# Decoder trunk on one core: the ramp's loads on two queues with casts in tile order, the last columns' residual added in the bank, and the down projection's loads asked for in order of use

## The chip, the cores and the metric

The kernel runs on one core of a Trainium2 chip. The time is device microseconds of one execution, from the device's own clock; lower is better. The engines are TensorE (PE, matmuls into PSUM banks; PEld is its loading of weights), VectorE (DVE), ScalarE (ACT), GpSimd (POOL) and SyncE (SP). DMAs are issued by SP, ACT or POOL, each with a queue of its own.

## The reference

A hybrid decoder trunk of one layer: 256 tokens behind 16 meta tokens (T = 272), width 2048, all in float32. Cut to what matters:

```python
u = rmsnorm(h, norm_mix)
proj = u @ w_in                               # q, k, v, gates of two groups of heads
ret = head_norm(retention(...), ret_norm) * silu(g_r)
hm = head_norm(mlstm(...), mlstm_norm) * sigmoid(o_m)
h = h + concat([ret, hm]) @ w_out
u = rmsnorm(h, norm_ffn)
gate, val = split(causal_dwconv(u @ w_up, ffn_conv_w, ffn_conv_b))   # FFN_DIM = 5632
h = h + (silu(gate) * val) @ w_down
out = rmsnorm(h, norm_final)[meta tokens dropped]
```

## The kernel before

Every float32 operand of a product is split into two parts of a rounded format: `whi` is the weight cast by ACT (L121), `wlo` the rest, raw minus `whi`, by DVE (L123); likewise `xh` and `xl`, `mh` and `ml`. A product is three matmuls: high x high (L130), low x high (L131) and high x low (L133). Weights come from HBM into `wraw`, a pool of four slots that all stages share; a load waits for a slot until the cast and the subtraction of the slot's last user are done. `whi` and `wlo` have five slots each. PSUM gives four banks `mmps` and four banks `atps`. The order of the instructions on each engine is set by a scheduler of the language at build time, from its own estimate of durations, from dependences, and from orders that the code gives (`issue_after`, `high_priority`); at run time each engine and each queue goes through its list in that order and waits where a semaphore says so.

The stages are: a ramp that projects k, q and the gates of the first heads straight from the inputs; the rest of the input projection with the two groups of heads; the output projection; and then, in two halves of the hidden units, up projection, convolution and gate, and down projection.

The ramp: `WARM` matmuls of `ones` (L199) keep PE busy before the first data. Then for k = 0, 1, and pairs (2,3), (4,5), ... SP loads 128 rows of the transposed input (`hT`) and of the first weights (`w0`, into `wraw`; for k = 0 and 1 on ACT's queue), ACT scales and casts `xh` (L219) and casts the weights of the pair in one instruction (L224), DVE makes `xl` (L220), `wlo` (L226) and the last 64 columns of `whi` (L227); PE does eight matmuls for each k (L130 to L133, L235, L236). `par` holds the norm's gains, without which no `xh` can be made.

The down projection goes, in each half, over two blocks b = 0 and 2, of two column tiles of 512 (b and b+1) and two row tiles each, and in each block over 11 steps q of two hidden tiles. Four steps (q = 0, 4, 9, 10) are plain: their `wd` weights are loaded for each of the two column tiles (L118), cast and multiplied with all four row and column combinations in `atps` (L827 to L830). The other seven (q = 1, 2, 3, 5 to 8) form a 2 x 2 product from seven products (`seven`, L859 to L862): one part of the weights (`kept`, 256 KB, worked out earlier) and three from HBM (`wd7`, 768 KB) are loaded into one of two areas `left`, which lie in `hT`, in turn; DVE forms differences `ta` (L844) and `tb` (L845) in two `wraw` slots; `split` (L764 on ACT, L766 on DVE) casts four operands, two from `hT` and two from `wraw`. Behind a block its seven-product banks are combined (`share`: L884 to L895) and the `atps` banks copied (L951), and POOL adds both to `hn` by accumulating DMAs (`hn<-x`, L878). In the last block of the second half the steps come in another order, and the last four plain steps of the second column tile are kept back (`alone`), so that the row tiles end one after another.

The end: `add` (L900) adds a bank to the residual `hn`; `squares` (L694, ACT) sums the squares; `times_gain` (L698, POOL) multiplies by the last norm's gain; `gather` (L703, L704) and `finish` (L710 to L714) give the factor of the row, and `scale` (L721 with the gain, L723 without, L726 on ACT) and the DMAs `out` end the kernel. The last 512 columns of the second row tile are done as two halves of 256.

## Time and profile before

| | |
|---|---|
| median of 3 runs | 1207.33 us (1207.29 to 1207.91) |
| profiled execution | 1207.7 us, span 1205.9 us |
| PE, DVE, ACT, POOL busy | 1194.6, 971.5, 709.5, 162.8 us |
| mean DMA rate over the span | 218 GB/s |

The median and the profiled execution are different executions. The span runs from the first to the last event of the profile; 1.8 us of the profiled execution lie outside. A wait in the profile is a gap on one engine, put down to the semaphore that came last; a chain goes back from the last instruction to whatever released it.

### The profile page before, as it was taken

Reading aid. Unit: us, or ns where it says so; the run is one execution under the profiler, and the core shown is the slowest. Engines: PE = TensorE matmul, PEld = TensorE weight load, DVE = VectorE, ACT = ScalarE, POOL = GpSimd, SP = SyncE. Lnnn points to the kernel's source line nnn. Section 1 sums busy time; section 2 is a strip of 40 time slices with the busy share of each in tenths; the row PEclk is TensorE's granted clock in tenths of the full one; section 3 lists DMA queues with packets and bytes.
Section 4 is the critical chain, followed back from the end, with each engine's and each line's share of the span. In section 5 each row is a group of like instructions: output and inputs, shape, how many; then the busy total and the mean of one; then the engine's idle time right before and its main releaser. Section 6 shows DMA issues by size and latency. Waiting matters only on the chain.

```text
span 1205.9 us, 22794 instructions
## 1 busy us (share of the span) xinstructions
PE 1194.6 (99%) x8956; PEld 1151.2 (95%) x8956; DVE 971.5 (81%) x1444; ACT 709.5 (59%) x963; POOL 162.8 (14%) x223
## 2 busy tenths in 40 slices
PE   9999999999999999999999999999999999999997
PEld 9999999999999999999999998878999999998886
DVE  8968788766775966789889879897788778789897
ACT  8747656655656646555555557664555555556664
POOL 0100001111110311021122100202022112100232
PEclk9999999999999999999999999999999999999999
DMA  8765555666565965766766834959787777755956
GB/s 278 269 212 164 170 184 170 197 183 192 169 192 165 349 200 175 252 220 212 253 219 214 279 117 175 278 177 276 284 251 255 223 240 249 261 176 211 274 181 186
DMA packets 83004, 263.27 MB, mean 218 GB/s; under 512 B 14672, under 2 KB 18896, under 8 KB 82768
## 3 DMA queue, kind: packets, MB, share of 16 engines
q1 hardware_dynamic: 71952, 223.85, 57.0%
q0 software_dynamic: 10368, 37.11, 10.1%
q8 instruction: 70, 1.15, 0.4%
q10 hardware_dynamic: 576, 0.85, 0.2%
q14 instruction: 38, 0.31, 0.1%
HBM read 243.42 MB, written 11.27 MB: 211 GB/s over the span
## 4 chain that ended last, share of the span: by engine, by line
PE 96%; DMA 2%; DVE 1%; ACT 0%; issue 0%; SPq 0%; DVEq 0%; ACTq 0%
PE mmps L130 26%; PE mmps L131 25%; PE mmps L133 25%; PE atps L827 2%; PE atps L828 2%; PE atps L830 2%; PE mmps L860 2%; PE mmps L862 2%; PE mmps L859 2%; PE atps L862 1%; PE atps L860 1%; PE atps L859 1%; DMA hn<-x 1%; PE atps L379 1%; DMA hT<-in_wd 1%; PE atps L371 0%
## 5 line engine op out<-in xcount | busy, mean ns | idle before, releaser
L121 ACT CAST whi<-wraw 128x1024 fp32r<-128x1024 f32 x352 | 369.3, 1050 | 342.0 <-PE mmps L131 228.7
L123 DVE TENSOR_TENSOR wlo<-wraw,whi 128x1024 fp32r<-128x1024 f32 x352 | 432.3, 1230 | 72.5 <-ACT whi L121 70.0
L130 PE MATMUL mmps<-uh,whi 128*128 128x258 f32 x1408 | 346.1, 283 | 0.0
L131 PE MATMUL mmps<-ul,whi 128*128 128x258 f32 x1408 | 346.0, 283 | 0.0
L130 PEld LDWEIGHTS mmps<-uh,whi 128*128 128x128 f32 x1408 | 267.6, 190 | 0.1
L131 PEld LDWEIGHTS mmps<-ul,whi 128*128 128x128 f32 x1408 | 267.1, 190 | 0.1
L130 PE MATMUL mmps<-xh,whi 128*128 128x272 f32 (+2 forms) x864 | 219.8, 288 | 0.0
L131 PE MATMUL mmps<-xl,whi 128*128 128x272 f32 (+2 forms) x864 | 218.3, 286 | 0.0
L133 PE MATMUL mmps<-uh,wlo 128*128 128x258 f32 x1408 | 196.5, 282 | 0.0
L133 PEld LDWEIGHTS mmps<-uh,wlo 128*128 128x128 f32 x1408 | 179.9, 189 | 0.0
L131 PEld LDWEIGHTS mmps<-xl,whi 128*128 128x128 f32 x864 | 162.8, 188 | 0.0
L130 PEld LDWEIGHTS mmps<-xh,whi 128*128 128x128 f32 x864 | 162.5, 188 | 0.1
L133 PE MATMUL mmps<-xh,wlo 128*128 128x272 f32 (+2 forms) x864 | 126.7, 285 | 0.0
L133 PEld LDWEIGHTS mmps<-xh,wlo 128*128 128x128 f32 x864 | 114.2, 188 | 0.0
L680 DVE TENSOR_TENSOR cu<-mmps,rstd 128x258 f32<-128x258 f32 x88 | 37.4, 425 | 55.3 <-PE mmps L133 54.8
L764 ACT CAST whi<-hT 128x1024 fp32r<-128x1024 f32 x52 | 53.6, 1052 | 27.2 <-PE atps L828 7.3
L766 DVE TENSOR_TENSOR wlo<-hT,whi 128x1024 fp32r<-128x1024 f32 x52 | 62.1, 1220 | 4.9 <-ACT whi L764 3.7
L131 PE MATMUL mmps<-mixl,whi 128*128 128x258 f32 x256 | 63.0, 283 | 0.0
L130 PE MATMUL mmps<-mixh,whi 128*128 128x258 f32 x256 | 62.4, 282 | 0.0
L764 ACT CAST whi<-wraw 128x1024 fp32r<-128x1024 f32 (+1 forms) x52 | 43.0, 838 | 16.8 <-PE mmps L860 6.8
L766 DVE TENSOR_TENSOR wlo<-wraw,whi 128x1024 fp32r<-128x1024 f32 (+1 forms) x52 | 52.2, 1037 | 0.6 <-PE mmps L862 0.2
L827 PE MATMUL atps<-whi,mh 128*128 128x512 f32 (+1 forms) x132 | 50.9, 387 | 1.3 <-ACT whi L121 1.1
(280 smaller groups left out, 1700.1 us busy)
## 6 DMA issues: line engine op xcount, KB each, us to landing
wraw<-in_wu SPq DMA_DIRECT2D x176, 512.0 KB, 4.4
wraw<-in_wi SPq DMA_DIRECT2D x108, 512.0 KB, 4.1
hT<-in_wd SPq DMA_DIRECT2D x26, 768.0 KB, 4.7
wraw<-in_wd SPq DMA_DIRECT2D x36, 512.0 KB, 4.7
wraw<-in_wo SPq DMA_DIRECT2D x32, 512.0 KB, 4.2
x<-in_wd POOLq DMA_DIRECT2D x13, 768.0 KB, 7.0
hn<-x POOLq DMA_DIRECT2D x27, 256.0 KB, 7.9
hT<-kept SPq DMA_DIRECT2D x26, 256.0 KB, 2.9
```

What stands on the lines that cost most here:

```text
L121: nc.scalar.copy(hi, raw)
L123: nc.vector.tensor_tensor(out=lo, in0=raw, in1=hi.bitcast(F32), op=ALU.subtract)
L130: nc.tensor.matmul(ps, hi[:, k, :], xh(kk), start=kk == first, stop=False)
L131: nc.tensor.matmul(ps, hi[:, k, :], xl(kk), start=False, stop=False)
L133: nc.tensor.matmul(ps, lo[:, k, :], xh(kk), start=False, stop=kk == last)
L680: evacuated = nc.vector.tensor_tensor(out=u, in0=ps[:, :NQ], in1=rstd2, op=ALU.mult)
L764: copied = nc.scalar.copy(hi, x)
L766: return copied, nc.vector.tensor_tensor(out=lo, in0=x, in1=hi.bitcast(F32), op=ALU.subtract)
L827: nc.tensor.matmul(ps, ah[i], hi[:, i, cols], start=first and i == 0, stop=False)
L859: nc.tensor.matmul(o, sh[:, f, m, :], hi[:, i, :], start=begin, stop=False)
L860: nc.tensor.matmul(o, sl[:, f, m, :], hi[:, i, :], start=False, stop=False)
L862: nc.tensor.matmul(o, sh[:, f, m, :], lo[:, i, :], start=False, stop=end)
```

## The change

In the ramp, the loads of the first three groups (k = 0, 1 and the pair 2, 3) are asked for at the start: `hT` on SP, the weights and, behind the first, `par` on ACT's queue. The weights of k = 0 to 3 are cast tile by tile, each directly behind its `xh`; k = 0's cast is done by DVE. A one-column copy on ACT stands ahead of the first `xh`. `WARM` goes from 8 to 7, and the memset of `ones` is the first on DVE. In the down projection every load of a stage is asked for behind the one before it, in the order in which the steps use them (`asked`). At the end the bank `pa1` of the last 256 columns gets one matmul, then the residual by a DVE add (L994 in the new file), then the rest of its matmuls; ACT squares it where it stands and `finish` scales from it; the gain of the 256 columns ahead of it is applied in `scale`, not by POOL.

```diff
@@ -32,7 +32,7 @@
 W0 = GW + 2 * P
-WARM = 8
+WARM = 7
@@ -104,18 +104,17 @@
     inv_dm = consts.tile([P, P], F32, name="inv_dm")
-    nc.vector.memset(inv_dm, 1.0 / DM)
     epsc = consts.tile([P, 1], F32, name="epsc")
-    nc.vector.memset(epsc, EPS)
     rstd2 = consts.tile([P, NQ], F32, name="rstd2")
...
-    def load_w(src, shape, to=None):
+    def load_w(src, shape, to=None, after=None):
         nonlocal last_load
         raw = wpool.tile(shape, F32, name="wraw", bufs=4)
-        last_load = nc.sync.dma_start(raw, src)
+        with tc.issue_after(after.ins) if after else nullcontext():
+            last_load = nc.sync.dma_start(raw, src)
         to, n = (wpool, 5) if to in (None, wpool) else (to, None)
@@ -169,6 +168,8 @@
     nc.vector.memset(ones, 1.0)
+    nc.vector.memset(inv_dm, 1.0 / DM)
+    nc.vector.memset(epsc, EPS)
     inv_ret = pa.tile([P, P], F32R, name="inv_ret")
@@ -204,27 +205,41 @@
     with pool("sq", 1, side="right") as sqp:
-        for k0, k1 in [(0, 1), (1, 2)] + [(k, k + 2) for k in range(2, KT, 2)]:
+        chunks = [(0, 1), (1, 2)] + [(k, k + 2) for k in range(2, KT, 2)]
+
+        def ask(k0, k1):
+            nonlocal last_load
+            nc.sync.dma_start(hT[:, k0:k1, :], io["xT"][:, k0:k1, :])
+            raw = wpool.tile([P, 2, W0], F32, name="wraw", bufs=4)[:, : k1 - k0, :]
+            load = (nc.scalar if k0 < 4 else nc.sync).dma_start(raw, io["w0"][:, k0:k1, :])
+            if k0 == 0:
+                nc.scalar.dma_start(par[:, 0:KT], io["par"][:, 0:KT])
+            if k0 >= 4:
+                last_load = load
+            return raw, load
+
+        asked = {c: ask(*c) for c in chunks[:3]}
+        with tc.issue_after(asked[chunks[2]][1].ins):
+            copied = nc.scalar.copy(rstd1[:, 0:1], ones[:, 0:1])
+        for k0, k1 in chunks:
             n = k1 - k0
-            nc.sync.dma_start(hT[:, k0:k1, :], io["xT"][:, k0:k1, :])
-            if k0 == 0:
-                nc.sync.dma_start(par[:, 0:KT], io["par"][:, 0:KT])
...
-            for k in range(k0, k1):
-                nc.scalar.activation(xh[:, k, :], hT[:, k, :], AF.Copy, scale=pcol("gmix", k))
-                nc.vector.scalar_tensor_tensor(out=xl[:, k, :], in0=hT[:, k, :], scalar=pcol("gmix", k),
-                                               in1=xh[:, k, :].bitcast(F32), op0=ALU.mult, op1=ALU.subtract)
-
+            raw, _ = asked[k0, k1] if (k0, k1) in asked else ask(k0, k1)
             hi = wpool.tile([P, 2, W0 + GW], F32R, name="whi", bufs=5)[:, :n, :]
-            copied = nc.scalar.copy(hi[:, :, 0:W0], raw)
             lo = wpool.tile([P, 2, 2 * P], F32R, name="wlo", bufs=5)[:, :n, :]
-            nc.vector.tensor_tensor(out=lo, in0=raw[:, :, 0 : 2 * P], in1=hi[:, :, 0 : 2 * P].bitcast(F32), op=ALU.subtract)
-            parted = nc.vector.tensor_tensor(out=hi[:, :, W0:], in0=raw[:, :, 2 * P :], in1=hi[:, :, 2 * P : W0].bitcast(F32), op=ALU.subtract)
+            for c0, c1 in [(0, 1), (1, 2)][:n] if k0 < 4 else [(0, 2)]:
+                for k in range(k0 + c0, k0 + c1):
+                    with tc.issue_after(copied.ins) if k != 1 else nullcontext():
+                        nc.scalar.activation(xh[:, k, :], hT[:, k, :], AF.Copy, scale=pcol("gmix", k))
+                if k0 == 0:
+                    nc.vector.tensor_copy(hi[:, c0:c1, 0:W0], raw[:, c0:c1])
+                else:
+                    copied = nc.scalar.copy(hi[:, c0:c1, 0:W0], raw[:, c0:c1])
+                nc.vector.tensor_tensor(out=lo[:, c0:c1], in0=raw[:, c0:c1, 0 : 2 * P], in1=hi[:, c0:c1, 0 : 2 * P].bitcast(F32), op=ALU.subtract)
+                for k in range(k0 + c0, k0 + c1):
+                    with tc.issue_after(parted.ins) if k >= 2 else nullcontext():
+                        nc.vector.scalar_tensor_tensor(out=xl[:, k, :], in0=hT[:, k, :], scalar=pcol("gmix", k),
+                                                       in1=xh[:, k, :].bitcast(F32), op0=ALU.mult, op1=ALU.subtract)
+                parted = nc.vector.tensor_tensor(out=hi[:, c0:c1, W0:], in0=raw[:, c0:c1, 2 * P :], in1=hi[:, c0:c1, 2 * P : W0].bitcast(F32), op=ALU.subtract)
             for k in range(k0, k1):
@@ -703,7 +718,7 @@
-    def finish(tt, n):
+    def finish(tt, n, end=None):
@@ -713,12 +728,12 @@
         rows = slice(tt * P, (tt + 1) * P)
-        late = DM - 256 if n == 4 else DM - 512
+        late = DM - 512
...
             if c0 >= late:
-                nc.vector.scalar_tensor_tensor(out=h, in0=h, scalar=t, in1=gfin[:, c0:c1], op0=ALU.mult, op1=ALU.mult)
+                nc.vector.scalar_tensor_tensor(out=h, in0=h if end is None or c0 < DM - 256 else end, scalar=t, in1=gfin[:, c0:c1], op0=ALU.mult, op1=ALU.mult)
             else:
@@ -728,9 +743,8 @@
             nc.sync.dma_start(out[rows, c0:c1], hn[:, tt, c0:c1])
-        for c0, c1 in ((1536, late), (late, DM)):
-            if c0 < c1:
-                scale(c0, c1)
+        for c0, c1 in ((1536, DM),) if end is None else ((1536, 1792), (1792, DM)):
+            scale(c0, c1)
         nc.sync.dma_start(out[rows, 1536:], hn[:, tt, 1536:])
@@ -739,7 +753,7 @@
     left = hT.rearrange("p k t -> p (k t)")[:, 0:4096].rearrange("p (i a n) -> i p a n", i=2, a=4)
-    turn = 0
+    turn, asked = 0, None
@@ -811,7 +825,7 @@
-        def product(ps, tt, q, w, first=False, last=False, c0=0):
+        def product(ps, tt, q, w, first=False, last=False, c0=0, n0=0, n1=6, seed=False, seeded=False):
@@ -823,22 +837,21 @@
                           for m, a in zip((sh, sl), a21))
-            for i in range(2):
-                nc.tensor.matmul(ps, ah[i], hi[:, i, cols], start=first and i == 0, stop=False)
-                nc.tensor.matmul(ps, al[i], hi[:, i, cols], start=False, stop=False)
-            for i in range(2):
-                nc.tensor.matmul(ps, ah[i], lo[:, i, cols], start=False, stop=last and i == 1)
+            parts = [(a[i], hi, i) for i in range(2) for a in (ah, al)] + [(ah[i], lo, i) for i in range(2)]
+            for n, (a, m, i) in list(enumerate(parts))[n0:n1]:
+                nc.tensor.matmul(ps, a, m[:, i, cols], start=first and n == 0, stop=seed or last and n == 5, skip_group_check=seeded)
...
-            nonlocal turn
+            nonlocal turn, asked
             f = FAST.index(q)
...
-            nc.sync.dma_start(raw[:, 0, :], early[b, q])
-            nc.sync.dma_start(raw[:, 1:4, :], io["wd7"][b // 2, half * NQD + q][:, 1:4, :])
+            for to, src in ((raw[:, 0, :], early[b, q]), (raw[:, 1:4, :], io["wd7"][b // 2, half * NQD + q][:, 1:4, :])):
+                with tc.issue_after(asked.ins) if asked else nullcontext():
+                    asked = nc.sync.dma_start(to, src)
             ta, tb = (wpool.tile([P, 2, 512], F32, name="wraw", bufs=4) for _ in range(2))
@@ -909,8 +922,12 @@
         def load_step(b, q, to=wpool):
-            return load_w(io["wd"][b, half * NQD + q], [P, 2, 512], to)
-
+            nonlocal asked
+            w = load_w(io["wd"][b, half * NQD + q], [P, 2, 512], to, asked)
+            asked = last_load
+            return w
+
+        asked = None
         lag = 4
@@ -969,16 +986,21 @@
             add(cs[1, 1], 1, c)
-            for i in range(2):
-                p = at.tile([P, 512], F32, name="atps")[:, 0:256]
-                for q in sorted(ws):
-                    product(p, 1, q, ws[q], q == alone[0], q == alone[-1], c0=i * 256)
-                add(p, 1, c + i * 256)
-                squares(1, 3 + i, c + i * 256, c + (i + 1) * 256)
-                if i == 0:
-                    times_gain(1, c, c + 256)
-                    gather(1, 4)
-            finish(1, 4)
+            qs = sorted(ws)
+            pa0, pa1 = (at.tile([P, 512], F32, name="atps")[:, 0:256] for _ in range(2))
+            h = hn[:, 1, c + 256 : DM]
+
+            product(pa1, 1, qs[0], ws[qs[0]], True, c0=256, n1=1, seed=True)
+            nc.vector.tensor_tensor(out=pa1, in0=pa1, in1=h, op=ALU.add)
+            for q in qs:
+                product(pa0, 1, q, ws[q], q == qs[0], q == qs[-1])
+            add(pa0, 1, c)
+            squares(1, 3, c, c + 256)
+            gather(1, 4)
+            for q in qs:
+                product(pa1, 1, q, ws[q], False, q == qs[-1], c0=256, n0=1 if q == qs[0] else 0, seeded=True)
+            nc.scalar.activation(junk[:, 0:256], pa1, AF.Square, scale=DM ** -0.5, accum_out=ss4[:, 1, 4:5])
+            finish(1, 4, pa1)
```

What this does to the order of the instructions is shown at three places.

ACT at the start of the ramp, before (L215 loads weights, L224 casts them, L219 makes `xh`):

```order
L215 DMA wraw_129<-in_w0 128x320
L215 DMA wraw_147<-in_w0 128x320
L224 ACT_TABLE_LOAD
L224 CAST whi_133<-wraw_129 128x320
L219 ACTIVATE xh_94<-hT_72,par_73 128x272
L224 CAST whi_151<-wraw_147 128x320
L219 ACTIVATE xh_94<-hT_72,par_73 128x272 x3
L224 CAST whi_171<-wraw_165 128x2x320
L219 ACTIVATE xh_94<-hT_72,par_73 128x272 x2
```

ACT there in the changed kernel:

```order
L214 DMA wraw_127<-in_w0 128x320
L216 DMA par_73<-in_par 128x16
L214 DMA wraw_131<-in_w0 128x320
L214 DMA wraw_134<-in_w0 128x640
L223 ACT_TABLE_LOAD
L223 COPY rstd1_92<-ones_86 128x1
L232 ACTIVATE xh_94<-hT_72,par_73 128x272 x2
L236 CAST whi_152<-wraw_131 128x320
L232 ACTIVATE xh_94<-hT_72,par_73 128x272
L236 CAST whi_167<-wraw_134 128x320
L232 ACTIVATE xh_94<-hT_72,par_73 128x272
```

ACT now issues four loads, the gains' among them, and no cast of k = 0; behind it `xh` and casts alternate tile by tile, where two `xh` and a cast of two tiles stood.

SP at the second block of the first half (`kept2_1` and `kept2_2` begin the loads of its q = 1 and 2; the six `in_wd` loads are two each for q = 9 and 10 of the first block and q = 0 of the second), before:

```order
L840 DMA hT_72<-kept2_1_6644 128x512
L841 DMA hT_72<-in_wd7 128x1536
L118 DMA wraw_9423<-in_wd 128x1024
L118 DMA wraw_9441<-in_wd 128x1024
L840 DMA hT_72<-kept2_2_6936 128x512
L841 DMA hT_72<-in_wd7 128x1536
L118 DMA wraw_9459<-in_wd 128x1024
L118 DMA wraw_9477<-in_wd 128x1024
L118 DMA wraw_9511<-in_wd 128x1024
L118 DMA wraw_9529<-in_wd 128x1024
```

SP there in the changed kernel:

```order
L117 DMA wraw_9426<-in_wd 128x1024
L117 DMA wraw_9444<-in_wd 128x1024
L117 DMA wraw_9462<-in_wd 128x1024
L117 DMA wraw_9480<-in_wd 128x1024
L117 DMA wraw_9514<-in_wd 128x1024
L117 DMA wraw_9532<-in_wd 128x1024
L854 DMA hT_72<-kept2_1_6647 128x512
L854 DMA hT_72<-in_wd7 128x1536
L854 DMA hT_72<-kept2_2_6939 128x512
L854 DMA hT_72<-in_wd7 128x1536
```

All plain loads, q = 9 and 10 of the first block and q = 0 of the second, now stand ahead of q = 1 and 2.

DVE a little later, with L844, L845 (L857, L858 in the new file) for `ta` and `tb` and L766 (L780) for `wlo`; the first two rows are q = 2, the last `ta` is q = 3:

```order
L844 TENSOR_TENSOR wraw_9592<-hT_72 128x1024
L845 TENSOR_TENSOR wraw_9593<-hT_72 128x512
L766 TENSOR_TENSOR wlo_9554<-hT_72,whi_9553 128x1024
L766 TENSOR_TENSOR wlo_9564<-hT_72,whi_9563 128x1024
L766 TENSOR_TENSOR wlo_9574<-wraw_9549,whi_9573 128x1024
L766 TENSOR_TENSOR wlo_9584<-wraw_9550,whi_9583 128x512
L766 TENSOR_TENSOR wlo_9597<-hT_72,whi_9596 128x1024
L766 TENSOR_TENSOR wlo_9607<-hT_72,whi_9606 128x1024
L844 TENSOR_TENSOR wraw_9635<-hT_72 128x1024
L845 TENSOR_TENSOR wraw_9636<-hT_72 128x512
L766 TENSOR_TENSOR wlo_9617<-wraw_9592,whi_9616 128x1024
L766 TENSOR_TENSOR wlo_9627<-wraw_9593,whi_9626 128x512
```

DVE there in the changed kernel:

```order
L857 TENSOR_TENSOR wraw_9595<-hT_72 128x1024
L858 TENSOR_TENSOR wraw_9596<-hT_72 128x512
L780 TENSOR_TENSOR wlo_9557<-hT_72,whi_9556 128x1024
L780 TENSOR_TENSOR wlo_9567<-hT_72,whi_9566 128x1024
L780 TENSOR_TENSOR wlo_9577<-wraw_9552,whi_9576 128x1024
L780 TENSOR_TENSOR wlo_9587<-wraw_9553,whi_9586 128x512
L780 TENSOR_TENSOR wlo_9600<-hT_72,whi_9599 128x1024
L780 TENSOR_TENSOR wlo_9610<-hT_72,whi_9609 128x1024
L780 TENSOR_TENSOR wlo_9620<-wraw_9595,whi_9619 128x1024
L780 TENSOR_TENSOR wlo_9630<-wraw_9596,whi_9629 128x512
L857 TENSOR_TENSOR wraw_9638<-hT_72 128x1024
```

The `ta` of q = 3 moved behind the four `wlo` of q = 2. The first two rows, `ta` and `tb` of q = 2, stand ahead of the `wlo` of q = 1 in both.

DVE at the end, before (L900, L913 in the new file: `add`; L703, L718: `gather`; L721 and L723, L736 and L738: `scale`):

```order
L900 TENSOR_TENSOR hn_4729<-atps_14072,hn_4729 128x256
L713 SCALAR_TENSOR_TENSOR frt_5853<-frt_5853,fr0_5852 128x1
L714 SCALAR_TENSOR_TENSOR frt_5853<-frt_5853,fr0_5852 128x1
L723 TENSOR_SCALAR hn_4729<-hn_4729,frt_5853 128x256
L723 TENSOR_SCALAR hn_4729<-hn_4729,frt_5853 128x768
L721 SCALAR_TENSOR_TENSOR hn_4729<-hn_4729,frt_5853,gfin_13139 128x512
L703 TENSOR_REDUCE rest_5851<-ss4_5848 128x1
L704 TENSOR_SCALAR rest_5851<-rest_5851 128x1
L900 TENSOR_TENSOR hn_4729<-atps_14102,hn_4729 128x256
L711 TENSOR_SCALAR frt_5853<-ss4_5848,rest_5851 128x1
```

DVE there in the changed kernel:

```order
L994 TENSOR_TENSOR atps_14076<-atps_14076,hn_4732 128x256
L913 TENSOR_TENSOR hn_4732<-atps_13617,hn_4732 128x512
L913 TENSOR_TENSOR hn_4732<-atps_14075,hn_4732 128x256
L726 TENSOR_SCALAR frt_5856<-ss4_5851,rest_5854 128x1
L728 SCALAR_TENSOR_TENSOR frt_5856<-frt_5856,fr0_5855 128x1
L729 SCALAR_TENSOR_TENSOR frt_5856<-frt_5856,fr0_5855 128x1
L718 TENSOR_REDUCE rest_5854<-ss4_5851 128x1
L738 TENSOR_SCALAR hn_4732<-hn_4732,frt_5856 128x256
L738 TENSOR_SCALAR hn_4732<-hn_4732,frt_5856 128x768
L736 SCALAR_TENSOR_TENSOR hn_4732<-hn_4732,frt_5856,gfin_13142 128x512
L719 TENSOR_SCALAR rest_5854<-rest_5854 128x1
L726 TENSOR_SCALAR frt_5856<-ss4_5851,rest_5854 128x1
```

The last add of 256 columns (`atps_14102`) is gone from behind the first row tile's scaling; the residual's add to `atps_14076` stands ahead of everything, and the reduction for the second row tile ahead of the first one's scaling.

5 lines of the change are left out of this document (removed).

## The prediction

> **What bounds the kernel.** I read the page's head first, then the list of everything that TensorE (PE) waited for, then the timelines around each entry of that list and around the end.
>
> ```profile
> span 1205.9 us, 22794 instructions
> PE 1194.6 (99%) x8956; PEld 1151.2 (95%) x8956; DVE 971.5 (81%) x1444; ACT 709.5 (59%) x963; POOL 162.8 (14%) x223
> ```
>
> PE is busy for 1194.6 of 1205.9 us, and the change takes no work from it but one warm-up call: as many product matmuls stand in it as before. So what can be won is the 11 us in which PE has no product to run: before the first one, in its waits, and after the last one. The waits of PE are a complete list of four (engine and line that waited, whom it waited for, total, count, longest):
>
> ```profile
> PE atps L199 <- DVE ones L171: 1.2, 1, 1.2
> PE atps L827 <- ACT whi L121: 1.1, 2, 0.7
> PE atps L130 <- ACT whi L224: 0.7, 1, 0.7
> PE atps L827 <- ACT x L951: 0.2, 1, 0.2
> ```
>
> The first and third lie in the ramp, the second and fourth in the down projection; the end of the kernel comes on top. The change touches all of them, so I price them one after the other. One change of this kernel can be told from none at about 0.2%, 2.4 us.
>
> **The ramp.** Columns: start, duration, engine, line, operation, tiles; in brackets the idle time before and its cause. The last four rows are from the chain (start, length, what).
>
> ```profile
> 1.21 3.79 PE L199 MATMUL atps<-ones 128*128 128x128 f32 x16 [1.21 <-DVE ones L171]
> 4.89 0.39 PE L130 MATMUL atps<-xh,whi 128*128 128x272 f32 x1
> 9.10 0.29 PE L130 MATMUL atps<-xh,whi 128*128 128x272 f32 x1
> 12.31 0.29 PE L130 MATMUL atps<-xh,whi 128*128 128x272 f32 x1
> ...
> 2.12 4.15 DMA hT<-in_xT
> 6.29 0.94 ACT xh L219 x2
> 7.24 0.73 ACT whi L224
> 8.02 0.39 PE atps L130
> ```
>
> From 9.10 to 12.31 lie 26 matmuls without a wait, 0.1235 us each. From 4.89 to 9.10 lie 22, which would take 2.72 of the 4.21 us: 1.49 us are waits. Most of it is the wait for k=2, whose weight cast (L224) ends at 7.97: it stands behind two `xh` of 0.47 each, which start when `hT` of k=2 and 3 lands (2.12 + 4.15 = 6.27), and it casts both tiles at once (0.73). The weights of the pair were asked for behind it on the same queue:
>
> ```profile
> 2.60 0.43 SPq L215 DMA_DIRECT2D wraw<-in_w  x1
> wraw<-in_w SPq DMA_DIRECT2D x1, 320.0 KB, 4.6
> 6.85 0.92 DVE L220 SCALAR_TENSOR_TENSOR xl<-hT,par,xh 128x272 fp32r<-128x272 f32 x2 [0.55 <-ACT xh L219]
> ```
>
> They land at 7.2. In the change one `xh` and a cast of one tile (estimate 0.44, half of 0.73 and a fixed part) stand there. With the landings as they are, k=2's cast ends at 7.2 + 0.44 = 7.65 in place of 7.97: 0.3 us. If they land 0.5 us sooner (they are ACT's fourth issue now and were SP's fifth, and an issue takes 0.43), it ends at 7.2: 0.8 us. The price stands on VectorE: k=0's cast moves there (an estimated 0.4, by ACT's 0.73 for twice the columns), and it gets two short operations per tile in place of two per pair (an estimated 0.1 for each one more). Its last row above has 0.55 of idle time just ahead of k=2, which covers the cast; the rest is paid when k=3 is as late on VectorE as on ACT. Bounds: 0.3 lost (VectorE late for k=3) and 1.3 won (no wait left but the first). I take 0.5, between the two landings, nearer to the one that the rows show. The earlier memset of `ones` moves only warm-up work.
>
> The Trainium skill, page "DMA: Bandwidth & Descriptors", section "Issuing engines are not separate DMA queues", says that queues of different engines end on the same 16 DMA engines and that only issue time is saved. By it the ramp's term would be the 0.3 us, and the sum 0.2 us smaller; here the rows of before show one queue at a time and can't decide it.
>
> **The down projection, half 0, second block.** The chain shows both what PE waited for and why:
>
> ```profile
> 777.29 1.23 DVE wlo L766
> 778.53 0.33 SPq L840
> 778.91 6.88 DMA hT<-in_wd
> 787.74 1.15 DVE wlo L766
> 788.90 3.52 DMA wraw<-in_wd
> 792.52 1.05 ACT whi L121
> ...
> 792.54 0.63 PE L862 MATMUL mmps<-wlo,sh 128*128 128x512 f32 x2
> 793.62 0.50 PE L827 MATMUL atps<-whi,mh 128*128 128x512 f32 x1 [0.45 <-ACT whi L121]
> ...
> 817.99 0.63 PE L862 MATMUL mmps<-wlo,sh 128*128 128x512 f32 x2
> 819.27 0.51 PE L827 MATMUL atps<-whi,mh 128*128 128x512 f32 x1 [0.65 <-ACT whi L121]
> ```
>
> A matmul of 512 columns follows the last after 0.23, so PE was due at 793.00 and began at 793.62: 0.62, and 0.11 more because the first after a wait lasts 0.50 and not 0.39. That is 0.73. The second: due at 818.45, began at 819.27, 0.82 + 0.11 = 0.93. Together 1.66 us.
>
> The first comes from VectorE's order. The plain step q=4 needs a `wraw` slot that the `wlo` at 787.74 frees; that one stood behind `ta` and `tb` of q=3 (L844, L845), which waited for a load of 6.88 us. In the changed order the four `wlo` of q=2 stand ahead of q=3's `ta`, so the slot no longer hangs on that load. But now the loads of q=1 and q=2 of this block are asked for behind those of q=0, and `ta` of q=2 stands ahead of the `wlo` of q=1. What that costs:
>
> ```profile
> 764.36 0.33 SPq L118 DMA_DIRECT2D wraw<-in_wd  x1
> 764.00:772.00 8.00, 8.00 (x37) 6.57 (x36) 7.59 (x10) 3.21 (x4) 3.40 (x4) 1.00 1.02 309
> 776.15 2.36 DVE L766 TENSOR_TENSOR wlo<-hT,whi 128x1024 fp32r<-128x1024 f32 x2
> 781.08 0.62 PE L862 MATMUL atps<-wlo,sh 128*128 128x512 f32 x2
> ```
>
> The last load of q=0 is asked for at 764.36; behind it now come 2 MB (q=1 and q=2, 1 MB each), with about 1 MB still open. The DMA engines moved 309 GB/s in that stretch (last column), part of it POOL's accumulating transfers of `hn<-x`; at an estimated 260 GB/s for SP's share, 3 MB take 11.5 us: q=2's weights land at about 776. `ta` and `tb` (787.74 - 785.79 = 1.95 with their start) then let the first `wlo` of q=1 run from 778.0 to 779.1; before, it ran from 776.15, and PE needs it at 781.08. So 2 us of slack are left. q=3's load, asked for when q=1's `wlo` has read its slot, goes out at about 780 in place of 778.53 and lands at 786 to 787 if POOL's transfers are done by then (785.8 before); PE comes to q=3 31 matmuls behind 781.08, at 788.2, and a cast of 1.05 lies between. That leaves next to nothing, and I charge 0.2 us. q=4's load goes out seven `wlo` behind 778.0 (1.15 each, one of half the size, and some waits for PE), at about 786.4 in place of 788.90; with 3.52 to 4 us it lands near 790.3, and its cast ends by 791.6, ahead of 793.0: 0.73 won. In the second stall the load of q=9 waits for a slot freed by q=7; the changed order puts that `wlo` ahead of q=8's `ta` and `tb`, nearly 2 us, and so its cast, which ended at 819.2, ends about 1 us before PE is due: 0.93 won. Bounds of the two: nothing (another wait takes their place) to 1.66. I take 1.66 - 0.2.
>
> **Half 1, end of its first block.**
>
> ```profile
> 1138.60 1.05 ACT L121 CAST whi<-wraw 128x1024 fp32r<-128x1024 f32 x1 [1.53 <-DMA wraw<-in_wd]
> 1138.96 1.07 PE L830 MATMUL atps<-wlo,mh 128*128 128x512 f32 x4
> 1140.19 0.50 PE L827 MATMUL atps<-whi,mh 128*128 128x512 f32 x1 [0.16 <-ACT x L951]
> ```
>
> Four at 0.23 make PE due at 1139.88; it began at 1140.19, and with 0.11 the loss is 0.42. It waits for a bank that ACT copies out (L951), and ACT was held until 1138.60 by a load for q=0. The change asks for that load ahead of the next block's 1 MB for q=2, worth 3.2 us on the queue at the 309 GB/s above, more than ACT's 1.53 of idleness. I take 0.4; bounds 0 and 0.42.
>
> At the start of each down projection the loads of q=1 and 2 now go out behind all up-projection weights. VectorE then waits an estimated 2 to 3 us in its order for them (1 MB at 309 GB/s behind the last load), with evacuations of `mmps` queued behind; PE has four such banks, and its first use of q=1 lies 5.5 us after the start of q=0. I cost this at nothing; if that cover is gone it is the slower rival below.
>
> **The end.**
>
> ```profile
> 1197.30 0.40 PE L830 MATMUL atps<-wlo,mh 128*128 128x256 f32 x2
> 1197.01 0.74 DVE L721 SCALAR_TENSOR_TENSOR hn<-hn,frt,gfin 128x512 f32<-128x512 f32 x1
> 1197.92 0.41 DVE L900 TENSOR_TENSOR hn<-atps,hn 128x256 f32<-128x256 f32 x1
> 1198.37 0.42 ACT L694 ACTIVATE junk<-hn 128x256 f32<-128x256 f32 x1 [1.91 <-DVE hn L900]
> 1199.92 1.15 DVE L723 TENSOR_SCALAR hn<-hn,frt 128x256 f32<-128x256 f32 x3
> 1200.98 0.48 DVE L721 SCALAR_TENSOR_TENSOR hn<-hn,frt,gfin 128x256 f32<-128x256 f32 x1
> ```
>
> PE ends at 1197.70; the add waits for VectorE's work on the first half of the rows (L721) until 1197.92, and the squares begin at 1198.37. In the change nothing stands between: squares at about 1197.74, 0.63 earlier, and everything behind them hangs on these. VectorE must have finished the other rows by 1198.3; before, they end at 1197.75, and its new order puts one reduction more ahead of them (an estimated 0.2). From the 0.63 goes 0.13: the third of the three L723 (1.15 for all, so about 0.35) becomes one of 0.48. Reading the bank in place of SBUF is not shown; the adds from a bank and the scaling from SBUF above have like durations (0.41, 0.48), so I put it at nothing, at most 0.2 either way. I take 0.5, bounds 0 and 0.8. The seeded add lies beside PE's 24 matmuls of the other half.
>
> **Sum.** 0.5 + 1.66 - 0.2 + 0.4 + 0.5 = 2.86 us. The profiled execution took 1207.7 (span 1205.9 and 1.8 around it), 0.4 above the median of 1207.33. Taken from the median: 1204.5.
>
> **Rivals.** (1) The loads' order moves the waits without removing them: PE then waits for q=3 or q=4 as before. For it: PE's slack at q=3 is next to nothing by my own numbers. Against: the slot that held q=4 is clearly freed earlier. Then 1.66 becomes about 0.4, the gain 1.6 to 1.9: 1205.6, no measurable change. (2) The clock stays low in the ramp. The 16 warm-up passes of the first row run into the first product; 14 of them (0.24 each) leave PE idle for about 0.4 us before it. If k=0 and 1 then run at half speed, 16 x 0.247 = 3.95 from 4.89, k=2 starts at 8.84, not 8.02: 0.8 lost in place of 0.5 won, sum 1.56, time 1205.8. The rows from 9.10 show full speed; no row shows what it takes. The Trainium skill, page "TensorE: Matmul & The Clock Gate", Part 1, has this rule: half clock until a free-running window of about 3.4 us was busy; no run here shows the threshold yet. (3) Slower: q=2's `ta` holds VectorE at the start of a second block. It decides from a landing at 778.0 (781.08 less 1.95 and 1.15); if POOL's transfers hold SP's as they did the load of 6.88 us, 5 us later than I count, PE loses 3 us there and 2 more on the load of q=3, and the waits at q=4 and 9 stay. With 0.5 + 0.4 + 0.5 won elsewhere that is 3.6 above before, 1210.9; with half the delay, 1208.4. Against it: of the two loads in the chain, one took 3.52 us. (4) All covers hold and the ramp loses all its waits: 1.3 there, 0.7 at the end, 4.1 in all: 1203.2.
>
> **Chances.** Forecast 0.50, (4) 0.09, (1) 0.22, (2) 0.11, (3) 0.08. The first two are faster by over 0.2%; (1) and (2) lie within; of (3) a quarter is within. So faster 0.59, same 0.35, slower 0.06. The range runs from (4)'s edge to past (1) and (2): 1203.4 to 1206.6, leaving out (3) and the far end of (4).
>
> **What would show it.** Ramp: k=2's first matmul at 7.2 to 7.7, all before it 0.12 apart. Half 0: no wait of PE on the L120 cast around 792 and 818; if wrong, a wait on the cast of `hT` near 788 or on `wlo` near 781. Half 1: no wait at 1139.9. End: squares of 256 columns within 0.1 us of PE's last matmul. The prediction fails if the list of PE's waits is as long as before with other names.

## The result and the profile after

The change made the kernel slower: median 1221.78 us (1220.04 to 1223.69), before 1207.55 us (1207.29 to 1207.91) in the same comparison; ratio 1.0118, 95% interval 1.0100 to 1.0136, so 14.2 us. The forecast was 1204.5, with a range of 1203.4 to 1206.6. The profiled execution took 1222.6 us (before 1207.7).

The head of the changed kernel's page:

```profile
span 1220.8 us, 22800 instructions
PE 1200.4 (98%) x8954; PEld 1151.1 (94%) x8954; DVE 970.4 (79%) x1447; ACT 705.2 (58%) x963; POOL 168.5 (14%) x222
```

Its list of PE's waits (who waited, for whom, us, times, longest):

```profile
PE atps L842 <- ACT whi L120: 3.1, 5, 1.2
PE atps L875 <- DVE wlo L780: 2.4, 1, 2.4
PE atps L132 <- DVE wlo L122: 1.7, 1, 1.7
PE atps L842 <- ACT x L968: 1.4, 2, 0.9
PE atps L872 <- ACT whi L778: 1.3, 1, 1.3
```

The list had four entries and now has nine (the four left out are 1.1, 0.6, 0.5 and 0.2); new are waits for VectorE's `wlo` and for casts of `hT`. PE's busy time grew too, by 5.8 us with no matmul more: matmuls at half speed, and more starts behind a wait.

At equal numbers of PE's matmuls the two traces show where the time goes. The changed kernel is 3.1 us behind at the start of the down projections, loses 6.4 more in half 0's and 6.0 more in half 1's, and gains 0.7 behind PE's last matmul.

**The down projection.** VectorE's own waits (same view, engine DVE, 728 to 795 us, half 0), before and after:

```profile
DVE wraw L844 <- DMA hT<-in_wd: 3.7, 2, 2.9
```

```profile
DVE wraw L857 <- DMA hT<-in_wd: 11.0, 6, 3.9
```

`ta` (L844, now L857), VectorE's first work for a seven-product step, now waits 11.0 us in all for its weights. VectorE's timeline in the changed kernel, two waits of the first block and the longest of the second:

```profile
742.80 1.23 DVE L857 TENSOR_TENSOR wraw<-hT 128x1024 f32<-128x1024 f32 x1 [0.95 <-DMA hT<-in_wd]
...
753.06 1.23 DVE L857 TENSOR_TENSOR wraw<-hT 128x1024 f32<-128x1024 f32 x1 [1.55 <-DMA hT<-in_wd]
754.20 0.69 DVE L858 TENSOR_TENSOR wraw<-hT 128x512 f32<-128x512 f32 x1
754.80 1.22 DVE L780 TENSOR_TENSOR wlo<-hT,whi 128x1024 fp32r<-128x1024 f32 x1
...
788.57 1.23 DVE L857 TENSOR_TENSOR wraw<-hT 128x1024 f32<-128x1024 f32 x1 [3.94 <-DMA hT<-in_wd]
```

At 753.06 the `ta` of q = 7 has waited; behind it stands, at 754.80, the last `wlo` of the step before that reads `hT`. That one frees the area into which q = 8's weights are loaded. So a late load makes VectorE wait, VectorE's wait keeps an area full, and the next load is asked for late: the waits renew themselves.

**The ramp.** PE's timeline:

```profile
5.01 0.59 PE L129 MATMUL atps<-xh,whi 128*128 128x272 f32 x1 [0.59 <-ACT xh L232]
...
5.62 0.43 PE L250 MATMUL atps<-xh,whi 128*128 128x272 f32 x1
...
8.91 0.43 PE L250 MATMUL atps<-xh,whi 128*128 128x272 f32 x1
...
9.34 0.29 PE L129 MATMUL atps<-xh,whi 128*128 128x272 f32 x1
```

VectorE's timeline behind the ramp:

```profile
23.95 1.27 DVE L270 TENSOR_TENSOR sum<-sum,turns 128x1088 f32<-128x1088 f32 x1
25.23 0.43 DVE L300 TENSOR_TENSOR g<-atps,g 4x272 f32<-4x272 f32 x1
25.68 0.43 DVE L299 COPY qT<-atps 4x272 f32<-4x272 f32 x1
26.04 2.34 DVE L122 TENSOR_TENSOR wlo<-wraw,whi 128x1024 fp32r<-128x1024 f32 x2
```

Sixteen products run 0.22 apart (0.43 each), and only from 9.3 us they are 0.12 apart (0.29 each). Then PE waits 1.7 us for the first projected tile's `wlo` (L122), which VectorE makes at 26.04, behind a sum of 1.27 (L270) and two short operations for the gates. Before, these three did not stand ahead of it:

```profile
22.78 2.34 DVE L123 TENSOR_TENSOR wlo<-wraw,whi 128x1024 fp32r<-128x1024 f32 x2
```

Of the 3.1 us by which the changed kernel is then behind, 1.2 come from the ramp and the rest from this wait.

**The end** (ACT in the chain) is as forecast: PE's last matmul ends at 1213.26, the squares from the bank (L1002) start at 1213.29, and from PE's end to the span's end it is 7.6 us, before 8.2.

```profile
1208.25 5.02 PE atps L842 x38
1213.27 0.02 issue
1213.29 0.03 ACT junk L1002
```

### The profile page after: what moved, and what is told of

It is laid out like the page before. It is cut to its first block, busy times and chain, and to the rows that moved or that the text cites. A ratio compares the mean times of both kernels' runs of the same rounds, so it can differ in the third digit from the quotient of the medians.

```text
span 1220.8 us, 22800 instructions
## 1 busy us (share of the span) xinstructions
PE 1200.4 (98%) x8954; PEld 1151.1 (94%) x8954; DVE 970.4 (79%) x1447; ACT 705.2 (58%) x963; POOL 168.5 (14%) x222
## 5 line engine op out<-in xcount | busy, mean ns | idle before, releaser
L122 DVE TENSOR_TENSOR wlo<-wraw,whi 128x1024 fp32r<-128x1024 f32 x352 | 434.9, 1238 | 69.4 <-ACT whi L120 67.8
L780 DVE TENSOR_TENSOR wlo<-hT,whi 128x1024 fp32r<-128x1024 f32 x52 | 61.7, 1223 | 2.0 <-ACT whi L778 2.0
L891 POOL DMA_DIRECT2D hn<-x x27 | 23.4, 908 | 210.0 <-ACT x L897 172.7
L842 PE MATMUL atps<-whi,ml 128*128 128x512 f32 (+1 forms) x132 | 50.7, 386 | 0.0
```

Source lines behind the costliest of these rows:

```text
L122: nc.vector.tensor_tensor(out=lo, in0=raw, in1=hi.bitcast(F32), op=ALU.subtract)
L780: return copied, nc.vector.tensor_tensor(out=lo, in0=x, in1=hi.bitcast(F32), op=ALU.subtract)
L842: nc.tensor.matmul(ps, a, m[:, i, cols], start=first and n == 0, stop=seed or last and n == 5, skip_group_check=seeded)
L891: nc.gpsimd.dma_start(block(tt, b), x, accum_op=ALU.add)
```

## The experiments

Four sets, each with its own runs of the kernel before, whose medians were 1207.45, 1206.90, 1207.13 and 1207.65 us. The difference is against that median, the interval is of the ratio.

| run | median, us | difference | ratio, 95% |
|---|---|---|---|
| e1 loads' order alone | 1222.16 | +14.7 | 1.0107 to 1.0143 |
| e2 ramp alone | 1212.37 | +4.9 | 1.0025 to 1.0052 |
| e3 end alone | 1205.98 | -1.5 | 0.9983 to 1.0001 |
| e4 e1, q = 1, 2 free | 1216.88 | +9.4 | 1.0066 to 1.0091 |
| e5 q = 5 behind q = 4 | 1211.53 | +4.6 | 1.0020 to 1.0044 |
| e6 q = 1, 2 held back | 1210.18 | +3.3 | 1.0017 to 1.0040 |
| e7 e1, no accumulation | 1216.86 | +10.0 | 1.0067 to 1.0093 |
| e8 e1, `ta` last | 1211.72 | +4.8 | 1.0024 to 1.0050 |
| e9 e2, `wlo` first | 1209.64 | +2.5 | 1.0017 to 1.0038 |
| e10 e9, loads as before | 1207.75 | +0.6 | 1.0001 to 1.0018 |
| e11 e3, `ta` last | 1205.94 | -1.2 | 0.9980 to 0.9997 |
| e12 e10 and e11 | 1206.82 | -0.3 | 0.9988 to 1.0006 |
| e13 e4 and e8 | 1207.94 | +0.3 | 0.9991 to 1.0008 |
| e14 all, repaired | 1208.64 | +1.0 | 0.9998 to 1.0015 |
| e15 e9, `WARM` = 9 | 1210.05 | +2.4 | 1.0010 to 1.0031 |

**e1 to e3: each part alone.** The kernel before with the hunks of one part of the diff: those with `asked` in `load_w`, `seven` and `load_step`; those of the ramp; those of `finish`, `product` and the end.

> Only the order of the down projection's loads is taken over; ramp and end are as before. Theory A (the three parts add up, each with the excess that the changed kernel shows in its stretch: 6.4 us between 740 and 835, 6.0 between 1140 and 1210): 1219 to 1220.5 us. Theory B (the parts work on each other: the late ramp shifts the loads against VectorE's order, and the order of the loads by itself does what the prediction said): 1205.5 to 1206.

> Only the ramp is taken over. Theory A (additive; 1.4 us of the excess before 20 us, 2.0 between 20 and 40 us): 1210.5 to 1211. Theory B (the wait of 1.7 us at 25 us, for a subtraction behind other work of VectorE, is made up later by work that is due anyway): 1208.5 to 1209. The prediction of the ramp's term would be 1206.8.

> Only the end is taken over. The prediction's term: 0.5 us won, 1206.8 to 1207.1. The traces by theory A: 0.6 to 0.9 won. Rival: the squares from the bank start early, but the output DMA's landing sets the end, 1207.3 to 1207.6 (nothing won).

Theory A held for the signs and roughly for the sizes (e1 and e2 lie 1.7 and 1.4 us above its ranges), theory B fell: the order of the loads costs 14.7 us with ramp and end untouched. In e2's profiled execution the ramp and the wait behind it cost 2.4 us by the start of the down projection. The rest of its loss lies behind that, where its code is that of before: PE waits 2.6 us there, before 1.3, and in e3, with the same code again, 0.2. So such waits vary between executions; whether the late ramp adds to them isn't shown. The three sum to 18.1 and the changed kernel lost 14.2, so they do not quite add up; which of them overlap isn't shown either. The end's gain has an interval that just reaches 1.

**e4: the loads of q = 1 and 2 asked for early again.**

```
- with tc.issue_after(asked.ins) if asked else nullcontext():
-     asked = nc.sync.dma_start(to, src)
+ with tc.issue_after(asked.ins) if asked and not (b == 2 and q <= 2) else nullcontext():
+     load = nc.sync.dma_start(to, src)
+ if not (b == 2 and q <= 2): asked = load
```

> As e1_loads, but the loads of q = 1 and 2 of each second block are left out of the chain, so that they are asked for as early as before the change (q = 1 ahead of q = 9's plain loads, q = 2 ahead of q = 10's); the loads inside the blocks keep the order of use. Theory A1 (the late loads of q = 1 and 2 are what costs: the wait of 2.8 us at 789 and what stands behind it): the stretch from 780 to 835 loses its excess, 2 to 4 us less than e1_loads. Theory A2 (the order inside the first block, with seven-product loads queued on SP behind plain loads that wait for a slot, is what costs; 760 to 770): no more than 1 us less than e1_loads, and the waits at 760 to 770 stay.

Both causes are real. e1's longest wait (4.4 us, PE L864 on VectorE's `wlo`, ending at 789.8) is gone, and e4 is 5.3 us faster; 9.4 remain, with waits of 2.5 us in all between 762 and 772 and of 4.0 in half 1.

**e5 and e6: the two changes of order one at a time, in half 0 only**, on the kernel before.

```
+ with tc.issue_after(last_load.ins) if (half, b, q) == (0, 0, 5) else nullcontext():          # e5
+ with tc.issue_after(last_load.ins) if (half, b) == (0, 2) and q in (1, 2) else nullcontext(): # e6
      nc.sync.dma_start(raw[:, 0, :], early[b, q])
      nc.sync.dma_start(raw[:, 1:4, :], io["wd7"][b // 2, half * NQD + q][:, 1:4, :])
```

> The kernel before with one change: in the first block of half 0 the loads of q = 5 (1 MB, seven-product step) are asked for behind the two plain loads of q = 4, as the order of use has it, not ahead of them. Theory C (VectorE has next to no slack in this block; its differences for q = 5 and 7 then wait about 2 us each for their load, with the subtractions of earlier steps queued behind, the area of q = 8 comes free some 6 us later, and PE waits between 750 and 770): 1209 to 1211 us, with 2 to 4 us of new waits there. Theory D (half 0's loss is all from the late loads of q = 1 and 2 of the second block): 1207 to 1208, no new wait ahead of 770.

> The kernel before with one change: the loads of q = 1 and 2 of half 0's second block (2 MB) are asked for behind all plain loads of q = 9, 10 and 0, as the order of use has it. Theory D (they then meet POOL's eight accumulating transfers; VectorE waits in its order for q = 2's weights, as rival 3 said): 1211 to 1213, one wait of PE of 3 to 5 us near 785 to 789. Theory C (the order inside the first block is the main cost, these loads have their 2 us of slack): 1207.5 to 1209, with waits below 1 us.

One swap of two neighbouring loads costs 4.6 us. VectorE in e5:

```profile
747.26 1.23 DVE L845 TENSOR_TENSOR wraw<-hT 128x1024 f32<-128x1024 f32 x1 [1.74 <-DMA hT<-in_wd]
...
749.00 1.22 DVE L766 TENSOR_TENSOR wlo<-hT,whi 128x1024 fp32r<-128x1024 f32 x1
...
755.16 1.23 DVE L845 TENSOR_TENSOR wraw<-hT 128x1024 f32<-128x1024 f32 x1 [0.93 <-DMA hT<-in_wd]
```

Theory C's chain is there, but PE does not pay at 750 to 770 in small waits: it pays once, 3.4 us up to 772.1, for a plain step's cast. e6 cost 3.3 us, between what the two theories gave. VectorE waited 3.34 us for q = 2's weights at 779.17, as theory D says, yet PE lost only 0.2 us there: its list has 1.4 for banks' copies and 1.1 for q = 4's cast, at 795.5. This execution is at the fast end of e6's range (1208.98 us), so where the slower ones lose more isn't shown. In e1, where VectorE comes to this place already late, PE loses 4.4 us.

**e7: without the accumulating transfers** of half 0's first block. This kernel leaves their sums out of its output; it is for the time alone.

```
+ if half == 1 or b > 1:
      nc.gpsimd.dma_start(block(tt, b), x, accum_op=ALU.add)
```

> As e1_loads, but the eight accumulating transfers behind half 0's first block are left out (their sums are missing from the output). Theory E (these transfers hold the 2 MB of q = 1 and 2 up): q = 2's weights land 5 to 8 us after they are asked for, not 16, the wait near 785 to 790 goes, 3 to 6 us less than e1_loads; the waits at 750 to 770 stay. Theory F (2 MB behind the plain loads are late by themselves): no more than 1 us less than e1_loads.

From issue to landing (min, median, max) of the four loads of q = 1 and 2 in e1, then of the last three of them in e7:

```profile
DMA to landing us min/median/max: 8.3/12.6/16.3
```

```profile
DMA to landing us min/median/max: 6.5/6.8/8.6
```

Theory E held: the longest, 16.3 us, became 8.6, the wait at 785 to 790 is gone, and with it 4.7 us of e1's 14.7.

**e8: the same loads, another order on VectorE.**

```
+ with tc.issue_after(rest_lo.ins) if rest_lo else nullcontext():
      nc.vector.tensor_tensor(out=ta, ...)
...
- copied, _ = split(hi[:, :n, :], lo[:, :n, :], w)
+ copied, rest_lo = split(hi[:, :n, :], lo[:, :n, :], w)
```

> As e1_loads, but on VectorE the differences (ta, tb) of each seven-product step are put behind the last subtraction of the step before, so that a late load no longer holds up work that is ready. Theory G (the cost is made on VectorE, which waits in its order): the area of q = 8 comes free about 4 us earlier, and half or more of e1_loads' loss goes: 1210 to 1215. Theory H (the loads' late landings alone make the waits): 1220 to 1223, as e1_loads.

This is the clearest of the runs: 9.9 of the 14.7 us go, with each load still asked for in the same order. VectorE in the first block:

```profile
743.82 1.22 DVE L847 TENSOR_TENSOR wraw<-hT 128x1024 f32<-128x1024 f32 x1
744.95 0.69 DVE L848 TENSOR_TENSOR wraw<-hT 128x512 f32<-128x512 f32 x1
745.55 2.35 DVE L767 TENSOR_TENSOR wlo<-hT,whi 128x1024 fp32r<-128x1024 f32 x2
747.83 1.82 DVE L767 TENSOR_TENSOR wlo<-wraw,whi 128x1024 fp32r<-128x1024 f32 x2
749.56 1.22 DVE L847 TENSOR_TENSOR wraw<-hT 128x1024 f32<-128x1024 f32 x1
...
761.05 2.35 DVE L124 TENSOR_TENSOR wlo<-wraw,whi 128x1024 fp32r<-128x1024 f32 x2
763.68 0.69 DVE L889 TENSOR_TENSOR x<-mmps,x 128x512 f32<-128x512 f32 x1 [0.28 <-ACT x L887]
```

From 743.82 to 763.4 VectorE has no bracket, and this gives the number that the prediction lacked. A seven-product step takes VectorE 5.74 us (743.82 to 749.56); PE's 21 matmuls at 0.23 take 4.8. A plain step takes VectorE 2.35 and PE 24 x 0.23 = 5.5. By these rows VectorE needs over a block 7 x 5.74 + 4 x 2.35 + 2.8 (four like L889) = 52.4 us, PE 7 x 4.8 + 4 x 5.5 = 55.6. So VectorE has an estimated 3 us to spare in a block; three waits of 0.95, 1.55 and 0.96 use that up in the changed kernel's first block.

**e9, e10 and e15: the ramp's parts.** e9 puts the two `wlo` ahead of the gates' copies again; e10 also sends the loads as before and has `WARM` = 8; e15 is e9 with two warm-up calls more.

```
+ with tc.issue_after(last_lo.ins):                                            # e9
      nc.vector.tensor_copy(o, gates_ps[g : g + MH, :T])
- load = (nc.scalar if k0 < 4 else nc.sync).dma_start(raw, ...)                 # e10
+ load = (nc.scalar if k0 < 2 else nc.sync).dma_start(raw, ...)
- nc.scalar.dma_start(par[:, 0:KT], ...)
+ nc.sync.dma_start(par[:, 0:KT], ...)
- WARM = 7
+ WARM = 8
```

> As e2_ramp, but on VectorE the two subtractions of the first projected tile stand ahead of the gates' copies and sums, as they did before. Theory I (the wait of 1.7 us at 25 us is VectorE's order, and nothing later gives it back): the wait goes, about 2 us less than e2_ramp, 1209.5 to 1210.5. Theory J (PE is then held at the next tile, whose load is as late): less than 0.5 us gained. In both, k = 1 and 2 still wait for weights that land at 6.3 and 7.7.

> As e9_wlo, but the loads go out as before the change (gains second on SP, weights of k = 2 and 3 on SP, WARM = 8); only the casts stay in tile order. Theory K (two queues share the same transfers, so weights on ACT's queue and the inputs on SP's land in a mixed order; in one order k = 1's weights land at 4.3 and k = 2's at 7.2): the ramp then has 0.3 to 0.5 us less waiting than before the change, 1206.5 to 1207.2 in all. Theory L (the tile-order casts themselves cost, by VectorE's extra work): 1208 or more.

> e9_wlo with WARM = 9, so that the warm-up matmuls end at about 5.05 us and no gap is left ahead of the first product at 5.0 to 5.2. Theory M (the gap of 1.0 to 1.2 us costs full speed in part of the executions, until 9.1 to 9.6): matmuls 0.125 apart from 6.5 us at the latest, 0.5 to 1 us less than e9_wlo. Theory N (full speed comes at the same time whatever the warm-up): 0.22 apart until 9, and the same time as e9_wlo within 0.3 us.

Theory I held: the wait at 25 us is gone and e9 is 2.4 us nearer to before than e2. With the loads' old queues and `WARM` = 8, e10 is 1.9 us nearer still. At the start of the down projection e2's trace is 2.4 us behind before, e9's 1.0 and e10's 0.3; so 1.4 and 0.7 of these gains lie in the stretch that was changed, and the rest isn't traced. ACT waits for the weights of k = 1 and 2 in e2:

```profile
6.29 0.46 ACT L235 CAST whi<-wraw 128x320 fp32r<-128x320 f32 x1 [0.95 <-DMA wraw<-in_w]
...
7.74 0.46 ACT L235 CAST whi<-wraw 128x320 fp32r<-128x320 f32 x1 [0.57 <-DMA wraw<-in_w]
```

PE in e10, the first matmul of k = 2 and the first of the first projected tile:

```profile
7.56 0.39 PE L128 MATMUL atps<-xh,whi 128*128 128x272 f32 x1
...
22.34 0.39 PE L128 MATMUL atps<-xh,whi 128*128 128x272 f32 x1 [0.17 <-ACT whi L119]
```

With the old queues k = 2 starts at 7.56, 0.46 sooner than before the change (8.02): the casts in tile order do what theory K says, though k = 2's weights also land 0.2 sooner in this execution. Of the 0.46, 0.2 is left at the last ramp products (21.01, before 21.23), and then the first projected tile's cast isn't ready: 22.34, before 22.22. The ramp's end is set by that tile's weights, so nothing remains: theory K was right on the place and wrong on the time. e15 has no gap and full speed from 5.7 us, as theory M says, but PE then waits 0.83 us for k = 1's weights at 7.35, and its time can't be told from e9's, as theory N says.

**e11 and e12: can it be made faster?** e11 is the kernel before with the new end and e8's order on VectorE; e12 has e10's ramp too.

> The kernel before with the new end, and with VectorE's differences (ta, tb) behind the last subtraction of the step before; the loads' order as before. If VectorE's order is what holds slots and areas (theory G), the waits at 793 and 818 shrink too: 1204.5 to 1206. Rival: the order was chosen for the step's own first product, so the new order makes ACT and PE wait for ta's cast: 1206.5 to 1209.

> The new end, casts in tile order with the loads in the old order (as e10_oneorder), and ta behind the last subtraction: if all three hold, 1203.5 to 1205.5, faster than both kernels. Rival: any of them moves VectorE's order elsewhere, and a new wait of 1 to 2 us takes its place, 1206 to 1207.5.

e11 is, with e3, the fastest of all: 1205.94, 0.03 to 0.20% faster than before. PE's whole list of waits in it:

```profile
PE atps L199 <- DVE ones L171: 1.2, 1, 1.2
PE atps L130 <- ACT whi L224: 0.8, 1, 0.8
```

Both lie in the ramp; the down projection has none left. But e3, with VectorE's old order, had only 0.2 us there and a median of 1205.98, so it isn't shown that the new order adds anything to the new end. e12 is no better: it came out as its rival said, and the new ramp adds a wait of 0.4 us for the first projected tile's cast (22.42).

**e13 and e14: is the account complete?** Both repairs on e1; and the changed kernel with these, e10's ramp and the new end.

> e1_loads with both repairs: ta and tb behind the last subtraction of the step before (e8), and the loads of q = 1 and 2 of the second blocks out of the chain (e4). If the two make up the loss of e1_loads: 1206.5 to 1208.5. If the order of use inside the blocks costs by itself: 1210 to 1212, with waits of PE at the plain steps.

> The changed kernel with all repairs (those of e13, and the ramp of e10 with its loads in one order, WARM = 8 and the first tile's subtractions first). If the account is complete: the sum of e13, e10 (+0.6) and the end (-0.9 to -1.5), 1206 to 1208. Rival: parts of the change work on each other and leave 2 us or more over that.

e13 is at the time of before, so nothing else in the order of the loads costs more than about 1 us. e14 has all parts of the change but the ramp's queues and `WARM` = 7, and is within 0.15% of before: the repairs account for about 13 of the 14.2 us. Its median is 0.6 us above the range expected, and its profiled execution, the slowest of its twelve, still loses 4.2 us between 740 and 772, around one wait of 2.2 us; so the repairs have not taken every such wait from every execution.

## Why the prediction was wrong

**The step that failed first is the sum for half 0** (1.66 - 0.2 won; 6.4 us lost). It followed two waits of PE and the loads right ahead of them. Those two waits are indeed gone in the changed kernel, but they are gone as well in e3's execution, which has the old order: part of what was to be won was the scatter of one execution. And the sum did not ask what every reordered load does to the engine that consumes it. q = 5's load behind q = 4's was not priced at all, and it alone costs 4.6 us (e5). VectorE's spare time, an estimated 3 us in a block of 55, could have been counted from the kernel and the rows of `ta` and `wlo`; the page's 81% share hid it, being a mean over stages.

**Rival 3 named the mechanism, at a chance of 0.08.** It set the point of decision at a landing of q = 2's weights at 778.0; in the changed kernel `ta` starts at 788.57, on the landing. The forecast had 11.6 us from q = 0's last load to that landing (764.36 to 776); it took 16.8, and that last load was itself asked for 7.3 us later, at 771.67. The estimate had taken 260 GB/s for SP's share. e7 shows the missing price: with POOL's eight transfers of 256 KB the longest of these loads takes 16.3 us in e1, without them 8.6. The one argument against the rival, that a load in the chain had taken 3.52 us, came from a stretch without such transfers.

**Half 1 (0.4 won; 6.0 us lost) failed, as far as the runs show, for the same reason.** The term followed one load of q = 0 and left out what the order does to the seven-product steps. VectorE and ACT have waits for the seven-product weights there (1075 to 1210 us) in the changed kernel, and none before:

```profile
DVE wraw L857 <- DMA hT<-in_wd: 5.4, 5, 2.9
```

```profile
ACT whi L778 <- DMA hT<-in_wd: 9.3, 5, 2.5
```

At equal numbers of PE's matmuls e1 loses 8.1 us in half 1 and e8, with VectorE's other order, 2.8. No run changes half 1 alone.

**The ramp (0.5 won) failed in two steps.** The weights of k = 2 were to land at 7.2 or 0.5 sooner, and those of k = 1 had no price. In e2 they landed at 7.7 and 6.3, in the changed kernel's execution at 8.4 and 6.9; k = 1's are about 2 us later than before (4.3). ACT's cast of k = 1's weights before, then its casts for k = 1 and 2 in the changed kernel:

```profile
4.74 0.44 ACT L224 CAST whi<-wraw 128x320 fp32r<-128x320 f32 x1
```

```profile
6.90 0.46 ACT L236 CAST whi<-wraw 128x320 fp32r<-128x320 f32 x1 [1.54 <-DMA wraw<-in_w]
...
8.43 0.46 ACT L236 CAST whi<-wraw 128x320 fp32r<-128x320 f32 x1 [0.65 <-DMA wraw<-in_w]
```

k = 1's weights are asked for at 1.66 in place of 1.18, behind the gains, and land beside `hT` of k = 2 and 3, which SP asks for at 1.65. Before and in e2 the same six transfers (the first `hT`, two weights, the gains, `hT` of k = 1 and of k = 2 and 3) are in by 6.3; only who waits for the last one changed. The rate was nearly the same, 369 GB/s before and 364 after (last column, after the clock and the DMA share):

```profile
5.00:9.10 4.10, 3.42 (x22) 2.81 (x23) 3.32 (x10) 3.40 (x8) 0.00 (x0) 1.00 1.01 369
```

```profile
5.00:9.10 4.10, 3.85 (x15) 3.43 (x16) 2.05 (x6) 1.92 (x5) 0.00 (x0) 1.00 0.99 364
```

The Trainium skill, page "DMA: Bandwidth & Descriptors", section "Issuing engines are not separate DMA queues", says that transfers of all issuing engines share the 16 DMA engines and interleave; the landings side by side agree. The prediction weighed it and priced it at 0.2 us less gained; that the interleaving would put needed bytes behind later ones was missed. The other step is the one that was not taken: the order of VectorE behind the ramp, where `wlo` had moved behind the gates' work (a wait of 1.7 us; e9 against e2 is 2.4 by the medians).

**Rival 2 (the clock) came true beside it in its sign,** in two of the three executions with `WARM` = 7 that were profiled: products are 0.22 apart until 9.3 us (changed kernel) and 9.8 (e9). In e2, with the same ramp as the changed kernel, they are not: its second and third product are 0.13 apart. The granted clock in the rows above reads 1.00 all the same, so only the distances tell of it, and that the clock is the cause isn't shown. The slow products cost less than the rival's 0.8 us. At the 121st product the changed kernel is 0.7 us behind e2 (22.39 and 21.68), but its weights had also landed 0.6 to 0.7 later; e15, whose weights landed as late and whose products ran at full speed, is there at 22.25, 0.1 sooner. e9, with e2's landings and slow products, is there at 22.14, 0.5 behind e2.

**The end (0.5 won) was right** in mechanism and size: 0.7 us by the two traces, and e3's interval holds it. That e3's median shows 1.5 is more than the end gives: of the 2.0 us that its trace is shorter than that of before, 1.4 lie ahead of the end, where the code is the same.

## What to carry to other kernels

A load asked for "in order of use" isn't asked for in order of need: a load that has its buffer free should not stand behind one that waits for a slot, nor a first consumer that waits for a load ahead of ready work on an engine that takes its list in order. Before moving loads, add up the consumer's time per stage (here VectorE, an estimated 52.4 of 55.6 us); the waits that it can bear are that difference, not what its share of the whole span suggests. And look at every engine's order behind the place that was edited: the scheduler moved `wlo` in a stretch that the diff doesn't touch.

## What was not expected of the hardware

A long wait of PE can be paid twice. After e1's 4.4 us, the granted clock was 0.50 for 4.9 us (eighth figure; ahead of the DMA share and the rate), with matmuls 0.43 apart in place of 0.23:

```profile
789.80:794.70 4.90, 4.89 (x12) 3.83 (x13) 4.90 (x5) 2.71 (x3) 0.00 (x0) 0.50 0.60 199
```

e14 shows it after only 2.2 us; PE's timeline, then the same view of the clock:

```profile
765.06 0.50 PE L843 MATMUL atps<-whi,mh 128*128 128x512 f32 x1 [2.21 <-ACT whi L120]
...
767.46 0.63 PE L843 MATMUL atps<-whi,mh 128*128 128x512 f32 x1
```

```profile
766.00:770.00 4.00, 4.00 (x13) 3.10 (x12) 3.76 (x6) 1.54 (x3) 1.69 (x2) 0.58 1.01 362
```

The changed kernel's wait of 2.4 us that ends at 791.6 was not followed by it (matmuls 0.23 apart). So the length of the wait alone doesn't decide. The ramp scatters too: of 14 profiled executions with 8 or 9 warm-up calls none had more than 9 products ahead of the steady distance of 0.12, while the three with 7 had 4, 16 and 20. The Trainium skill, page "TensorE: Matmul & The Clock Gate", Part 1, gives a free-running window of about 3.4 us as the cause of such scatter. The ramp's scatter fits that, but no run here varies the window. Its rule that a clock closes after an idle window of that length does not fit e14, where 2.2 us of waiting was enough.
